# A hybrid decoder layer on one core: v after the scores, the first norm's place among the up products, and smaller moves

## The chip, the core and the metric

The kernel runs on one core of a Trainium2 chip. Its time is the device time of one execution in microseconds (us); of the three runs shown the median counts. The engines are TensorE (PE in the profile, with its weight loads as PEld), VectorE (DVE), ScalarE (ACT), GpSimd (POOL) and SyncE (SP), whose queue issues nearly all DMAs, in order. ACT, DVE and POOL, too, each run their instructions in the order in which the program gives them.

## The reference

One decoder layer for a prompt of 2048 tokens and 8 samples of 8 tokens: 2112 tokens of width 1024, in float32.

```python
# ada: scale, shift, gate for both norms from silu(c) @ w_ada
h = rmsnorm(x) * (1 + scale) + shift
qkv, z, b, a, sq, sk, sv = split(h @ w_in)        # one input projection
# (A) gated DeltaNet, 4 heads of 128: short causal conv, silu, q and k normalized,
decay = exp(G_i - G_j)                            # G: cumulated log decay
A = strict_lower(beta * (k @ k.T) * decay)        # scores k.k, and (q @ k.T) * decay
T = inverse(I + A)
u = T @ (beta * v) - T @ (beta * exp(G) * k) @ S  # state S goes from chunk to chunk
o = (q * exp(G)) @ S + (q @ k.T * decay) @ u
# (B) banded attention, window 128, with sinks and a position bias
x = x + gate * (concat(A, B) @ w_out)
h = rmsnorm(x) * (1 + scale2) + shift2
y = x + gate2 * ((silu(conv(h @ w_up_g)) * conv(h @ w_up_u)) @ w_down)
```

## The kernel before

A product in float32 is made of three products of halves: each factor is split into a rounded high part and the rest (hi and lo for the tokens, w_hi and w_lo for the weights), and `gemm_steps` adds hi·w_hi, lo·w_hi and hi·w_lo for eight k steps of 128, 24 matmuls in one PSUM bank (line 370 of the kernel; a matmul has up to 512 columns, the tokens). `split` (lines 361 and 362) casts the high part of a weight on ACT and subtracts for the low part, on DVE unless it is handed another engine. A weight piece w_raw of 512 KB has two buffers, and so have w_hi and w_lo: the next piece can only be loaded once the low part of the piece two before it is done.

The tokens are worked on in two halves, of two blocks of 512 and of blocks of 384, 384 and 320. In order of time the stages are: the ada modulations (`ada_cols`) and the input projection of the first half (`inproj`); the mixers of the first half, chunks of 128 tokens in four generators that advance side by side (`front` for the chunk two ahead, `levels` for the next, `scan` and `attend` for the chunk itself), with the input projection of the second half as a filler between their steps; `between(0)`, which is the output projection of the first half and its second norm; the mixers of the second half with the up-projection of the first as filler; the sample tokens (`sample_delta`, `sample_attend`); `between(1)`; the up-projection of the second half (`up_quarters`, a form with fewer products, whose weight sums are split in a ring of tiles); and the down-projection. `weight_sums` makes sums of pieces of the down weights for a product form with fewer products, from two loads of 512 KB, four additions of 128 by 512 and two stores (ws_d) for each of its eleven units; before, six run on POOL beside the input projection and five on DVE beside the sample tokens.

What sets the order: the generators say what is offered when (`beside(steps, filler, share)` takes `share` steps of the filler for each step), and a scheduler then puts every engine's instructions in one order. `tc.issue_after(x)` keeps what is issued inside it behind x.

`front` loads kq (keys and queries of a chunk) and xv (its values) from the tensor proj, to which the input projection stores through SP. It transposes kq for the squares (kq_ps), forms the decay Dc, transposes v and scales it to vb (lines 735 and 737), and then makes the scores AM (am_ps, two products of two heads each, and four operations on DVE), whose part AT is stored to at_d and read back as blocks G, from which DVE inverts 16 by 16 blocks. `levels` joins these to larger blocks, and `scan` reads vb.

A second norm goes through `ffn_in`: the squares are added up by token on ACT and POOL (line 1317, acc), `token_rstd` sums them over partitions on TensorE (ss_ps), takes the root (rsq on DVE, rtok on POOL), spreads it as diagonals (dg on DVE) and sends it back through TensorE (rb_ps), and `affine_h` scales the tokens and splits them into hi and lo (x at line 295, hi at 301 on ACT, lo at 302 on DVE and 299 on POOL). In the first half the norm of the last block runs beside the first up products, which use the other block.

In `between`, free PSUM banks are handed out in turn (`turns`), and `out_weights` keeps two split weights ahead of the output products.

## Time and profile before

| what | number |
|---|---|
| runs | 2584.51, 2585.77 and 2588.64 us, median 2585.77 |
| profiled execution | 2588.13 us, span 2586.4 us, mean granted clock of TensorE 0.994 |
| busy in the span | PE 97%, DVE 70%, ACT 50%, POOL 30% |
| input projection of the first half | up to about 242 us |
| mixers of the first half | about 387 to 745 us |
| output projection of the first half, norm | about 745 to 892 us |
| sample tokens | about 1290 to 1420 us |
| output projection of the second half | about 1531 to 1632 us |
| matmuls | 16410 |

Busy is the time in which an engine executes; a row of the timeline has the start in us, the duration, engine, line, operation and tiles, and in brackets the idle time of that engine before it with what ended it. Where an engine has no bracket, it did not wait. "x8" means that so many instructions are merged in the row. A granted clock of 0.50 in a stretch means that TensorE ran at half speed there.

### The profile page before, as it was taken

What the parts mean: (1) busy time and instruction counts of PE and PEld (TensorE: products, weight loads), DVE (VectorE), ACT (ScalarE), POOL (GpSimd) and SP (SyncE); (2) the same over time, 40 slices, a digit from 0 to 9 for tenths busy, and PEclk for the clock granted to TensorE, in tenths of its full rate; (3) what the DMA queues carried; (4) which work ended last, traced back from release to release, by engine and by line L of the source; (5) the groups of instructions that cost most, each with busy time, mean ns of one, the idle gap of its engine ahead of it and who ended that gap; (6) DMA issues with size and microseconds to landing.
All of it is one profiled execution on the core that took longest, in us unless ns stands there. A gap on an engine that the chain in (4) does not pass through costs nothing.

```text
span 2586.4 us, 45302 instructions
## 1 busy us (share of the span) xinstructions
PE 2515.8 (97%) x16410; PEld 2211.3 (85%) x16410; DVE 1811.4 (70%) x3621; ACT 1286.7 (50%) x3133; POOL 763.9 (30%) x697
## 2 busy tenths in 40 slices
PE   7999999999999999999999999999999999999998
PEld 5777888888988787787887789999999998888998
DVE  6465579897543677788758665886776666687676
ACT  5554365554343455465544353655555554454453
POOL 2064143323232422222111123345555520021012
PEclk9999999999999999999999999999999999999999
DMA  7887553343555353443346267325555448676463
GB/s 278 281 297 255 159 141 112 101 120 93 128 178 203 109 150 96 107 104 100 88 163 200 80 219 225 112 78 164 174 174 183 160 168 293 213 242 201 138 193 133
DMA packets 315852, 427.62 MB, mean 165 GB/s; under 512 B 82243, under 2 KB 206244, under 8 KB 315364
## 3 DMA queue, kind: packets, MB, share of 16 engines
q1 hardware_dynamic: 315052, 423.55, 51.8%
q8 instruction: 129, 2.11, 0.3%
q0 software_dynamic: 288, 1.11, 0.1%
q14 instruction: 95, 0.78, 0.1%
q10 hardware_dynamic: 288, 0.06, 0.0%
HBM read 305.07 MB, written 120.57 MB: 165 GB/s over the span
## 4 chain that ended last, share of the span: by engine, by line
PE 75%; DVE 11%; DMA 6%; ACT 3%; issue 2%; POOL 2%; SPq 1%; DVEq 0%; POOLq 0%; ACTq 0%
PE up_ps L370 19%; PE dn_ps L1850 17%; PE in_ps L370 8%; PE op_ps L370 6%; PE uq_b L1632 6%; PE uq_c L1632 3%; DVE ev L581 3%; PE uq_u L1632 2%; PE uq_g L1632 2%; PE uq_a L1632 1%; PE as_ps L1009 1%; DMA wada<-in_w_ada_dram 1%; PE pv_ps L1047 1%; PE u_ps L819 1%; DVE w_lo L362 1%
## 5 line engine op out<-in xcount | busy, mean ns | idle before, releaser
L370 PE MATMUL in_ps<-hi,w_hi 128*128 128x512 f32 (+2 forms) x880 | 319.4, 366 | 2.5 <-ACT hi L301 1.9
L370 PE MATMUL in_ps<-lo,w_hi 128*128 128x512 f32 (+2 forms) x880 | 315.6, 359 | 3.1 <-DVE lo L302 2.0
L370 PE MATMUL up_ps<-hi,w_hi 128*128 128x512 f32 (+2 forms) x808 | 313.0, 388 | 1.5 <-ACT sg L576 1.5
L370 PE MATMUL in_ps<-hi,w_lo 128*128 128x512 f32 (+2 forms) x880 | 314.0, 357 | 0.5 <-POOL w_lo L362 0.5
L370 PE MATMUL up_ps<-lo,w_hi 128*128 128x512 f32 (+2 forms) x808 | 312.1, 387 | 1.9 <-DVE lo L302 1.9
L370 PE MATMUL up_ps<-hi,w_lo 128*128 128x512 f32 (+2 forms) x808 | 311.0, 386 | 0.1
L1850 PE MATMUL dn_ps<-tl,wh 128*128 128x512 f32 (+2 forms) x796 | 271.6, 341 | 0.0
L1850 PE MATMUL dn_ps<-th,wh 128*128 128x512 f32 (+2 forms) x796 | 269.9, 341 | 0.0
L1850 PE MATMUL dn_ps<-th,wl 128*128 128x512 f32 (+2 forms) x796 | 268.7, 341 | 0.0
L361 ACT CAST w_hi<-w_raw 128x1024 fp32r<-128x1024 f32 x126 | 132.1, 1049 | 145.9 <-PE op_ps L370 63.0
L362 DVE TENSOR_TENSOR w_lo<-w_raw,w_hi 128x1024 fp32r<-128x1024 f32 x115 | 145.3, 1264 | 84.1 <-ACT w_hi L361 78.3
L370 PEld LDWEIGHTS in_ps<-lo,w_hi 128*128 128x128 f32 x880 | 166.9, 190 | 23.1 <-issue 3.4
L370 PEld LDWEIGHTS in_ps<-hi,w_hi 128*128 128x128 f32 x880 | 166.2, 190 | 23.2 <-issue 3.6
L370 PEld LDWEIGHTS up_ps<-hi,w_hi 128*128 128x128 f32 x808 | 152.3, 188 | 35.2 <-issue 7.3
L370 PEld LDWEIGHTS up_ps<-lo,w_hi 128*128 128x128 f32 x808 | 152.4, 189 | 33.4 <-issue 6.4
L370 PEld LDWEIGHTS in_ps<-hi,w_lo 128*128 128x128 f32 x880 | 166.5, 189 | 15.9 <-issue 1.0
L370 PEld LDWEIGHTS up_ps<-hi,w_lo 128*128 128x128 f32 x808 | 152.1, 188 | 27.9 <-issue 1.6
L1734 ACT CAST wh<-wr 128x512 fp32r<-128x512 f32 x149 | 92.2, 619 | 154.8 <-PE dn_ps L1850 101.6
L581 DVE SCALAR_TENSOR_TENSOR ev<-rb,cw,ev 128x512 f32<-128x512 f32 (+2 forms) x180 | 142.6, 797 | 35.2 <-ACT ev L574 31.5
L1850 PEld LDWEIGHTS dn_ps<-tl,wh 128*128 128x128 f32 x796 | 150.5, 189 | 15.7 <-DVE tl L1735 0.3
L1850 PEld LDWEIGHTS dn_ps<-th,wl 128*128 128x128 f32 x796 | 150.4, 189 | 15.2
L1850 PEld LDWEIGHTS dn_ps<-th,wh 128*128 128x128 f32 x796 | 150.2, 189 | 15.5
(574 smaller groups left out, 6414.6 us busy)
## 6 DMA issues: line engine op xcount, KB each, us to landing
w_raw<-in_w_upT_dram SPq DMA_DIRECT2D x50, 512.0 KB
wada<-in_w_ada_dram SPq DMA_DIRECT2D x48, 512.0 KB
w_raw<-in_w_inT_dram SPq DMA_DIRECT2D x44, 512.0 KB
wr<-ws_d SPq DMA_DIRECT2D x88, 256.0 KB
w_raw<-in_w_outT_dram SPq DMA_DIRECT2D x34, 512.0 KB
d<-act_d SPq DMA_DIRECT2D x33, 512.0 KB
wr<-in_w_downT_dram SPq DMA_DIRECT2D x66, 256.0 KB
proj<-ev SPq DMA_DIRECT2D x44, 256.0 KB
```

The costliest lines, as they stand in the source:

```text
L361: nc.scalar.copy(hi, raw)
L362: (eng or nc.vector).tensor_tensor(lo, raw, hi.bitcast(F32), ALU.subtract)
L370: nc.tensor.matmul(ps[:, :n], a[:, k, :], b[:, k, :n], start=first is not False and k == ks[0] and i == 0, stop=last is not False and k == ...
L581: nc.vector.scalar_tensor_tensor(out, src(j), w[:, j:j + 1], out, ALU.mult, ALU.add)
L819: mm = lambda out, a, b, r, c: nc.tensor.matmul(out, a, b, start=True, stop=True, tile_position=(r, c))
L1009: nc.tensor.matmul(banks[v][:, 256 * g:256 * g + 256 - P * k0], qs[:, 2 * (g0 + g) + v], t[:, v, :2 - k0].rearrange("p w j -> p (w j)"), s ...
L1047: mm = nc.tensor.matmul(pv_ps[64 * v:64 * v + 64, :], (vprev[0], vt if k0 else dv)[half][:, 64 * v:64 * v + 64], PT[v, half], start=half = ...
L1632: nc.tensor.matmul(bk[t][:, :nb], u[:, k], v[:, k], start=new and k == 0 and y == 0, stop=k == KG - 1 and y == 2, skip_group_check=True)
L1734: nc.scalar.copy(h, raw)
L1850: nc.tensor.matmul(acc[m, s][:, :n], w[q, i][a][:, c], th[b][:, v], start=new and i == 0 and y == 0, stop=i == KH - 1 and y == 2, skip_gro ...
```

## The change

Nothing that is computed changes. The edits are:

- `front`: the transposes of v and vb come after the scores, their store and the loads of G, instead of before them. The scheduler orders the mixers anew from that.
- `ada_init`: a Silu of 16 columns is issued first, so that ACT loads its table at the very start.
- `gates`: the exponential of al is issued behind the copy `held`.
- `weight_sums`: five units (FEW) on POOL beside the input projection and six on DVE beside the sample tokens.
- `between`: the output projection starts at the other bank (`turns[0] = 1`); in the first half, ss of the last block's norm stands behind six k steps (18 matmuls) of the up-projection and rb behind six more.
- `out_weights`: in the second half every second new split has its low part on POOL.
- `Quarters`: two further rings (RING_T) for the split weights instead of one; a copy of small constants becomes smaller for it.

On SP the first loads of kq move. Before, they stand here (the names are target and source of a DMA):

```order
L643 DMA proj<-ev 128x512 x2
L1685 DMA ws_d<-suv 128x1024 x2
L353 DMA w_raw<-in_w_inT_dram 128x1024
L691 DMA kq<-proj 128x4x128 x2
L693 DMA xv<-proj 128x4x128
```

and now:

```order
L360 DMA w_raw<-in_w_inT_dram 128x1024
L651 DMA proj<-ev 128x512
L699 DMA kq<-proj 128x4x128 x2
L701 DMA xv<-proj 128x4x128
L262 DMA he<-in_xT_dram 128x384 x2
```

The unit's stores ws_d are gone from ahead of kq, and the second of the two proj stores comes behind it; on TensorE the first kq_ps stands 33 matmuls of the input projection earlier.

On DVE the norm of the first half stood so, after the last split of the first up weights (sg and cv are conv taps of the up products):

```order
L581 SCALAR_TENSOR_TENSOR sg<-rb,fcw,sg 128x512 x2
L143 TENSOR_SCALAR rsq<-ss_ps 128x4
L599 SCALAR_TENSOR_TENSOR sg<-rb,sg 128x512
L223 TENSOR_SCALAR dg<-cst,rtok 128x128 x4
L581 SCALAR_TENSOR_TENSOR cv<-rb,fcw,cv 128x512 x2
L1350 SCALAR_TENSOR_TENSOR cv<-cv,sg 128x512
L295 SCALAR_TENSOR_TENSOR x_9223<-x_9223,MOD,rb_ps 128x512 x8
L302 SCALAR_TENSOR_TENSOR lo<-x_9223,MOD,hi 128x512 x2
```

and stands so now:

```order
L144 TENSOR_SCALAR rsq<-ss_ps 128x4
L230 TENSOR_SCALAR dg<-cst,rtok 128x128 x4
L589 SCALAR_TENSOR_TENSOR sg<-rb,fcw,sg 128x512 x2
L302 SCALAR_TENSOR_TENSOR x_9216<-x_9216,MOD,rb_ps 128x512 x3
L607 SCALAR_TENSOR_TENSOR sg<-rb,sg 128x512
L302 SCALAR_TENSOR_TENSOR x_9216<-x_9216,MOD,rb_ps 128x512 x5
L309 SCALAR_TENSOR_TENSOR lo<-x_9216,MOD,hi 128x512 x2
```

The norm's operations come ahead of the taps of the second up product, and of the first one's too. On TensorE, 36 up matmuls stood ahead of ss and 26 between ss and rb; now it is 18 and 18.

On POOL the start of the second half's output projection was only sums of squares (acc), the root and the token splits (lo):

```order
L1225 TENSOR_TENSOR mixl<-mt,mixh 128x320 x4
L1317 TENSOR_TENSOR acc<-acc,sq 128x384 x7
L144 TENSOR_TENSOR rtok<-rsq,mhalf 128x3
L1317 TENSOR_TENSOR acc<-acc,sq 128x384
L299 TENSOR_TENSOR lo<-ht,hi 128x384
```

Now the weight splits stand among them; this is its last third, from the root of the second block's norm on:

```order
L145 TENSOR_TENSOR rtok<-rsq,mhalf 128x3
L369 TENSOR_TENSOR w_lo<-w_raw,w_hi 128x1024
L1337 TENSOR_TENSOR acc<-acc,sq 128x320 x2
L369 TENSOR_TENSOR w_lo<-w_raw,w_hi 128x1024
L306 TENSOR_TENSOR lo<-ht,hi 128x384 x2
L1337 TENSOR_TENSOR acc<-acc,sq 128x320 x2
L306 TENSOR_TENSOR lo<-ht,hi 128x384
L369 TENSOR_TENSOR w_lo<-w_raw,w_hi 128x1024
L1337 TENSOR_TENSOR acc<-acc,sq 128x320
```

Nine splits of the output weights went from DVE's order to POOL's; a split stands ahead of the two lo's here.

The diff:

```diff
--- before.py
+++ after.py
@@ -4,6 +4,7 @@
 
 
 from contextlib import ExitStack, nullcontext
+from itertools import islice
 
 import numpy as np
 
@@ -154,6 +155,8 @@
         craw = tmp.tile([P, KT, 9], F32, tag="craw", name="craw")
         nc.scalar.dma_start(craw, I["cT"])
         cT = pool.tile([P, KT, 32], F32, tag="cT", name="cT")
+        warm = tmp.tile([P, 16], F32, tag="warm", name="warm")
+        nc.scalar.activation(warm, mhalf, AF.Silu)
         bT = pool.tile([P, 48], F32, tag="bT", name="bT")
         nc.vector.memset(cT, 0.0)
         nc.scalar.activation(cT[:, :, 0:9], craw, AF.Silu)
@@ -207,16 +210,20 @@
         yield True
 
 
+    asked = []
+
     def token_rstd(accs, n, dst, pool, bank):
 
 
         ps = bank("ss_ps")
         r = pool.tile([P, 4], F32, tag="rtok", name="rtok")
+        asked.clear()
 
         cuts = [min(t, n - P) for t in range(0, n, P)]
         for j, t in enumerate(cuts):
             for i, a in enumerate(accs):
-                nc.tensor.matmul(ps[:, j:j + 1], a[:, t:t + P], ones[:, 0:1], start=i == 0, stop=i == len(accs) - 1)
+                asked.append(nc.tensor.matmul(ps[:, j:j + 1], a[:, t:t + P], ones[:, 0:1], start=i == 0,
+                                              stop=i == len(accs) - 1).ins)
         rsqrt(pool, r[:, :len(cuts)], ps[:, :len(cuts)], 1.0 / D, len(cuts))
         dg = pool.tile([P, len(cuts), P], F32, tag="sq", name="dg", bufs=2)
         for j, t in enumerate(cuts):
@@ -224,7 +231,7 @@
         yield True
         bp = bank("rb_ps")
         for j, t in enumerate(cuts):
-            nc.tensor.matmul(bp[:, t:t + P], ones, dg[:, j], start=True, stop=True)
+            asked.append(nc.tensor.matmul(bp[:, t:t + P], ones, dg[:, j], start=True, stop=True).ins)
         if dst is not None:
             nc.scalar.copy(dst[:, :n], bp[:, :n])
         yield True
@@ -467,7 +474,7 @@
                     nc.tensor.matmul(pb[:32, :n], wb[:, k, :], h[bi][i][:, k, :n], start=i == 0 and k == 0,
                                      stop=i == 1 and k == KT - 1)
             ev = gw.tile([P, 512], F32, tag="cv", name="ba_ev", bufs=CV)
-            nc.scalar.copy(ev[:32, :n], pb[:32, :n])
+            held = nc.scalar.copy(ev[:32, :n], pb[:32, :n]).ins
             yield True
             ps = st_bank("bat_ps")
             for i, t in enumerate(range(0, n, P)):
@@ -484,7 +491,8 @@
         dt = pool.tile([P, H], F32, tag="dt", name="dt")
         nc.sync.dma_start(al, I["dn_A_log"][0].partition_broadcast(P))
         nc.sync.dma_start(dt, I["dn_dt_bias"][0].partition_broadcast(P))
-        nc.scalar.activation(al, al, AF.Exp)
+        with tc.issue_after(held):
+            nc.scalar.activation(al, al, AF.Exp)
         t0, t1, t2 = [pool.tile([P, NCH // 2 + 1, H], F32, tag=t, name=t)[:, :n_] for t in ("t0", "t1", "t2")]
         sl = slice(c1, c1 + n_)
 
@@ -730,13 +738,6 @@
             nc.vector.tensor_scalar_mul(nr[:rows, :, 0], nr[:rows, :, 0], 1.0 / f)
         nc.vector.tensor_scalar_mul(nr[:rows, :, 1], nr[:rows, :, 1], float(128.0 ** -0.5))
         yield True
-        v_ps = bank("v_ps", "fr")
-        for h in range(H):
-            nc.tensor.transpose(v_ps[:rows, P * h:P * h + P], xv[:, h, :], ident)
-        vb = pool.tile([P, H, P], F32, tag="vb", name="vb", bufs=two)
-        nc.vector.tensor_tensor(vb[:rows], heads(v_ps)[:rows], over_i(nr[:rows, :, 0], P), ALU.mult)
-        yield True
-
         AM = pool.tile([P, H, 2, rows], F32, tag="AM", name="AM", bufs=1 if smp else 2)
         for s in range(2):
             am_ps = bank(f"am_ps{s}", "fr")[:, :4 * rows].rearrange("p (h i t) -> p h i t", h=2, i=2)
@@ -759,6 +760,12 @@
         for h in range(H):
             nc.sync.dma_start(G[nb * h:nb * h + nb], bass.AP(a0.tensor, a0.offset + h * rows,
                                                              [[BS * ap_ + BS, nb], [ap_, BS], [1, BS]]))
+        yield True
+        v_ps = bank("v_ps", "fr")
+        for h in range(H):
+            nc.tensor.transpose(v_ps[:rows, P * h:P * h + P], xv[:, h, :], ident)
+        vb = pool.tile([P, H, P], F32, tag="vb", name="vb", bufs=two)
+        nc.vector.tensor_tensor(vb[:rows], heads(v_ps)[:rows], over_i(nr[:rows, :, 0], P), ALU.mult)
         yield True
         TU = pool.tile([4 * P // BS, 2, BS, BS], F32, tag="TU", name="TU", bufs=1)
         T0 = TU[:np_, 0]
@@ -1227,6 +1234,8 @@
 
 
 
+    FIRST_UP = (6, 6)
+
     OUT_ORDER = (tuple(range(KT)), (KT - 2, KT - 1, *range(KT - 3, -1, -1)), (1, 0, *range(2, KT)))
 
     def out_weights(hf):
@@ -1239,7 +1248,7 @@
                 del w[m]
                 new = next((x for x in seq[i + 1:] if x not in w), None)
                 if new is not None:
-                    w[new] = load_split(I["w_outT"][new])
+                    w[new] = load_split(I["w_outT"][new], nc.gpsimd if hf and i % 2 else None)
             yield
 
     def outproj(hf, bi, mix, sums, op, weights, kept=None):
@@ -1286,6 +1295,7 @@
         beside(chain(mix_load(hf, 0, mix, op), mix_load(hf, 1, mix, op)), filler, SHARE[4][hf])
         rest(filler)
         weights = out_weights(hf)
+        turns[0] = 1
         steps = outproj(hf, 0, mix, sums, op, weights)
         for bi in range(2, nb):
             beside(mix_load(hf, bi, mix, op), steps, 2)
@@ -1297,7 +1307,17 @@
             beside(ffn_in(hf, bi, h, sums, op), steps, SHARE[5])
             rest(steps)
         up = up_proj(hf, h, uc[0], op, ms)
-        beside(ffn_in(hf, nb - 1, h, sums, op, *kept), up, SHARE[6][hf])
+        normed = ffn_in(hf, nb - 1, h, sums, op, *kept)
+        if not hf:
+            next(normed)
+            rest(islice(up, FIRST_UP[0]))
+            with tc.issue_after(asked[-1]):
+                next(normed)
+                next(normed)
+                rest(islice(up, FIRST_UP[1]))
+            with tc.issue_after(asked[-1]):
+                beside(normed, up, SHARE[6][hf])
+        beside(normed, up, SHARE[6][hf])
         return up, h
 
     def residual(out, ps, n, np_, g, x, pool):
@@ -1425,7 +1445,7 @@
             halves_of("T4", b21, k)
             yield
 
-    RING, RING_T = 6, 1
+    RING, RING_T = 6, 2
 
     def quarter_tiles(pool, i):
         return [pool.tile([P, KG, P], F32R, tag=f"r{s}{i}", name=f"r{s}") for s in "hl"]
@@ -1433,7 +1453,8 @@
     def copy_consts(dst, src):
         for t in ("cw", "cb"):
             nc.gpsimd.tensor_copy(dst[t], src[t])
-        nc.gpsimd.tensor_copy(dst["out"][:, 2 * PLAIN:], src["out"][:, 2 * PLAIN:])
+        late = lambda a: a[:, a.shape[1] - MU + 2 * PLAIN:]
+        nc.gpsimd.tensor_copy(late(dst["out"]), late(src["out"]))
 
     class Quarters:
 
@@ -1927,6 +1948,7 @@
 
     SHARE = (5.4, 5.5, 4.0, 2.05, (2.0, 1.4), 5.0, (1.3, 2.0), 8.0)
     PLAIN = 3
+    FEW = 5
 
     gate = cp.tile([P, NCH + 1, H], F32, tag="gate", name="gate")
     ghl = cp.tile([P, 2, NCH + 1, H], F32R, tag="ghl", name="ghl")
@@ -2031,7 +2053,7 @@
         at_bank = lambda name: bank(name, "at")
         tasks = lockstep(
             chain(*[spaced(ada_cols([(c, k + q) for q in range(4)], ac, st, at_bank), 2) for c in range(2, 6) for k in (0, 4)],
-                  spaced(weight_sums(range(6), sa, nc.gpsimd), 2)),
+                  spaced(weight_sums(range(FEW), sa, nc.gpsimd), 2)),
             chain(bias_tables(sa), gates(0, h, ic["wb"], ip), *[x_rstd(1, bi, rBs[bi], sa, st_bank) for bi in range(3)]))
         zero_images(sa)
         filler = inproj(0, h, ic, range(2, 12), tags=("acc", "acc", "fr", "fr", "at"), turn=(0, 0), w0=w2)
@@ -2104,7 +2126,7 @@
         nc.sync.dma_start(O["p_ssm"].rearrange("h k v -> k h v"), state[0])
         with ExitStack() as es:
             sp = new_pool(es, "sp", side="right")
-            beside(lockstep(sample_delta(sp), sample_attend(sp), weight_sums(range(6, KH), sp, nc.vector)), filler, SHARE[2])
+            beside(lockstep(sample_delta(sp), sample_attend(sp), weight_sums(range(FEW, KH), sp, nc.vector)), filler, SHARE[2])
         with ExitStack() as es:
             up_tags[:] = FREE_TAGS
             filler, h = between(1, filler, es, range(2 * PLAIN))
@@ -2118,7 +2140,8 @@
                 ts = new_pool(es2, "ts", side="right")
                 beside(chain(token_sums(q, ts), W.first(PLAIN)), filler, SHARE[7])
                 rest(filler)
-            uc2 = {t: tq.tile(list(a.shape), F32, tag=f"u{t}", name=f"u{t}") for t, a in uc[0].items()}
+            shape = lambda t, a: [P, MU - 2 * PLAIN, 18] if t == "out" else list(a.shape)
+            uc2 = {t: tq.tile(shape(t, a), F32, tag=f"u{t}", name=f"u{t}") for t, a in uc[0].items()}
             copy_consts(uc2, uc[0])
             nc.sync.dma_start(O["ffn_conv"][:, :2 * PLAIN], uc[0]["out"][:, :2 * PLAIN])
             states.close()
```

## The prediction, made before the changed kernel was run

> **What bounds the kernel now.** I read the page first: its span and the busy shares.
>
> ```profile
> span 2586.4 us, 45302 instructions
> PE 2515.8 (97%) x16410; PEld 2211.3 (85%) x16410; DVE 1811.4 (70%) x3621; ACT 1286.7 (50%) x3133; POOL 763.9 (30%) x697
> ```
>
> TensorE is idle for 2586.4 − 2515.8 = 70.6 us in all. None of the edits removes a matmul, so whatever they win must come out of those 70.6 us, or out of matmuls that run at half clock behind a stall. Next I read the waits of TensorE; of that view these are three that the edits aim at (columns: waited for in total, times, the longest).
>
> ```profile
> PE kq_ps L705 <- DMA kq<-proj: 4.5, 1, 4.5
> PE op_ps L370 <- DVE w_lo L362: 2.4, 3, 1.3
> PE uq_b L1632 <- DVE rl L1488: 1.5, 1, 1.5
> ```
>
> At most 8.4 us can be won by these; two more stand in the timeline of the norm (1.49 and 1.91). Last, the table by stretches gives the stage of the first mixers, the one behind it, and the clock behind two of the stalls (columns: length, PE, PEld, DVE, ACT, POOL busy with counts, then the granted clock).
>
> ```profile
> 370.00:610.00 240.00, 221.45 (x1909) 200.21 (x1909) 208.72 (x604) 128.69 (x441) 77.32 (x79) 0.99 0.38 106
> 610.00:745.00 135.00, 135.00 (x1111) 126.61 (x1110) 72.07 (x227) 58.80 (x186) 33.98 (x36) 0.99 0.47 126
> 242.80:246.20 3.40, 3.40 (x13) 2.93 (x14) 1.46 (x3) 0.80 (x2) 0.00 (x0) 0.50 1.07 399
> 1072.20:1075.60 3.40, 3.40 (x10) 0.77 (x9) 3.30 (x17) 1.94 (x6) 2.66 (x3) 0.50 0.00 0
> ```
>
> Behind each of the two stalls TensorE ran 3.4 us at half clock, which costs 1.7 us more. From 370 to 610 it idles 240 − 221.45 = 18.55 us in many small waits; from 610 to 745, with the filler's last part, not at all.
>
> **The norm of the first half (next to the first up products).** Rows of the timeline of TensorE, POOL and DVE:
>
> ```profile
> 865.68 0.39 PE L370 MATMUL up_ps<-hi,w_hi 128*128 128x512 f32 x1
> 872.48 0.95 PE L219 MATMUL ss_ps<-ones,acc 128*128 128x1 f32 x8
> 879.41 1.05 PE L227 MATMUL rb_ps<-dg,ones 128*128 128x128 f32 x8
> 884.53 0.50 PE L370 MATMUL up_ps<-hi,w_hi 128*128 128x512 f32 x1 [1.49 <-ACT sg L576]
> 886.93 0.50 PE L370 MATMUL up_ps<-lo,w_hi 128*128 128x512 f32 x1 [1.91 <-DVE lo L302]
> 888.01 0.63 PE L370 MATMUL up_ps<-hi,w_lo 128*128 128x512 f32 x1
> 891.00 0.55 PE L370 MATMUL up_ps<-hi,w_hi 128*128 128x512 f32 x1
> 866.97 1.93 POOL L1317 TENSOR_TENSOR acc<-acc,sq 128x512 f32<-128x512 f32 x1 [4.81 <-ACT sq L1316]
> 875.14 0.88 DVE L223 TENSOR_SCALAR dg<-cst,rtok 128x128 f32<-128x128 f32 x4 [0.91 <-POOL rtok L144]
> 880.50 5.36 DVE L295 SCALAR_TENSOR_TENSOR x<-x,MOD,rb_ps 128x512 f32<-128x512 f32 x8 [0.60 <-PE rb_ps L227]
> 885.78 1.76 DVE L302 SCALAR_TENSOR_TENSOR lo<-x,MOD,hi 128x512 fp32r<-128x512 f32 x2
> ```
>
> From 865.68 to 872.48 stand 30 matmuls of 512 columns without a wait: one every 6.80/30 = 0.227 us. From 888.01 to 891.00 seven of them take 2.99 instead of 1.59 us: 1.4 lost to the clock. With 18 matmuls ahead of ss instead of 36, TensorE is there at 872.48 − 18 × 0.227 = 868.4; POOL ends the last sum at 868.9, so a new wait of 0.5 comes. ss to the end of dg took 876.02 − 872.48 = 3.54, so dg is done at 872.4. ss (0.95) and 18 more matmuls (4.1) put TensorE at rb at 874.0: no wait. The x operations follow 1.09 later, at 875.1 instead of 880.5. They take 5.36, one sg (0.7) is now among them, and the first lo (half of 1.76) is done at 882.0. rb (1.05) and the remaining 36 matmuls of the first token block last until 874.0 + 1.05 + 8.2 = 883.2, so lo is 1.2 early. The evacuation that held the bank (sg) is early too, since the fourth product now takes over a bank one product older. The gain is 1.49 + 1.91 + 1.4 − 0.5 = 4.3. Later lo's (spaced 0.9 on DVE against 0.68 per k step) may cost a little; I take **−4.0**, ends −4.7 and −2.5.
>
> **One unit of weight sums moved, and kq with it.** SP's timeline and the chain:
>
> ```profile
> 225.94 7.74 SPq L643 DMA_DIRECT2D proj<-ev  x2
> 236.86 1.47 SPq L691 DMA_DIRECT2D kq<-proj  x2
> 236.86 5.79 DMA kq<-proj
> 242.72 4.67 DMA proj<-ev
> 247.41 3.35 DMA kq<-proj
> 242.70 1.93 PE L705 MATMUL kq_ps<-cst,kq 128*128 128x128 f32 x8 [4.49 <-DMA kq<-proj]
> ```
>
> Before, kq stands in SP's queue behind a second proj store, two ws_d stores that wait for POOL, and a weight. Now it stands right behind the proj store that left at 225.94, and must wait for that store to land. A store took 4.67 and kq 5.79 or 3.35; with at least 2 us for a store in a quieter queue (an estimate from half of 4.67) kq lands between 231.6 and 236.4. But TensorE's order also has kq 33 matmuls earlier: it arrives at 238.2 − 33 × 0.227 = 230.7. So the wait is 0.9 to 5.7 us, in the middle 3.3 against 4.49. Half clock stays for a wait of some 2 us and more, as behind the stall ahead of 1072.2, which a row below shows to be 2.4. I take **−1.2**; the ends are −5.3 (wait 0.9, no half clock) and +1.2. The unit's four operations, 128 by 512 like vb's, go to DVE in the sample stage, where TensorE is busy 129.57 of 130 us:
>
> ```profile
> L737 DVE TENSOR_TENSOR vb<-v_ps,nr x17: 671/691/693, 263.1 to 1366.9; 128x512 f32<-128x512 f32 x16, 64x512 f32<-64x512 f32 x1
> 1290.00:1420.00 130.00, 129.57 (x749) 101.02 (x748) 93.70 (x202) 56.15 (x153) 19.83 (x14) 1.00 0.53 175
> ```
>
> 4 × 0.69 = 2.8 us of DVE with 36 free: 0; uncovered it would be 2.8.
>
> **Splits of the second half's output weights on POOL.**
>
> ```profile
> L362 POOL TENSOR_TENSOR w_lo<-w_raw,w_hi x11: 2374/2396/2795, 345.8 to 746.5; 128x1024 fp32r<-128x1024 f32 x11
> 1616.85 1.03 ACT L361 CAST w_hi<-w_raw 128x1024 fp32r<-128x1024 f32 x1
> 1618.88 3.34 POOL L299 TENSOR_TENSOR lo<-ht,hi 128x384 fp32r<-128x384 f32 x2 [3.20 <-ACT hi L298]
> 1626.03 1.05 ACT L361 CAST w_hi<-w_raw 128x1024 fp32r<-128x1024 f32 x1 [1.09 <-DMA w_raw<-in_w_outT_dram]
> 1628.95 0.41 PE L370 MATMUL op_ps<-mixh,w_lo 128*128 128x320 f32 x1
> SPq L294 <- POOL lo L299: 2.1, 1, 2.1
> ```
>
> Of the 2.4 that op_ps waited for w_lo, 0.42 is in the first half (below) and 2.0 here, in two waits; they should go, as DVE loses nine splits. But the last split is POOL's: its weight lands at 1626.0, w_hi ends at 1627.08, and 2.40 on POOL end at 1629.5, where TensorE used it at 1628.95. Also POOL's lo of 1618.88, for which SP's queue waits with ht ahead of that weight (the last row), now stands behind a split that starts at w_hi's end, 1617.88, and lasts to 1620.3: 1.4 later, and the weight as much. So the stage ends 0.5 to 1.9 later, though no wait before it is left; if the weight comes as much earlier as the waits removed, it ends 1.5 earlier. I take **+0.7**, ends −1.5 and +1.9.
>
> **The other edits.** The second split ring removes the 1.49 at uq_b, but DVE's sums on either side of that split are unmoved, so about half comes back: **−0.7** (−1.5 to 0). The first output product of a half in another bank no longer waits for ev, by the rows:
>
> ```profile
> 770.22 1.45 DVE L362 TENSOR_TENSOR w_lo<-w_raw,w_hi 128x1024 fp32r<-128x1024 f32 x1 [6.43 <-ACT w_hi L361]
> 771.72 0.70 PE L370 MATMUL op_ps<-mixh,w_lo 128*128 128x512 f32 x1 [0.42 <-DVE w_lo L362]
> ```
>
> TensorE can start when w_hi is there, which DVE's split needs too, so at 770.2 (ev would have been waited for until 770.56), but its third matmul still waits for w_lo until 771.7: **0** (−0.3 to 0). The early table load takes 1.28 us from ahead of the squares:
>
> ```profile
> 5.86 1.28 ACT L159 ACT_TABLE_LOAD   x1
> 14.87 1.23 DVE L362 TENSOR_TENSOR w_lo<-w_raw,w_hi 128x1024 fp32r<-128x1024 f32 x1 [2.80 <-ACT w_hi L361]
> 16.01 0.16 DVE L143 TENSOR_SCALAR rsq<-ss_ps 128x4 f32<-128x4 f32 x1
> ```
>
> But rsq stands behind a split whose weight sets its time, and DVE's order there is unchanged: **0** (−1.3 to 0). The load ahead of al hides under the same work: 0.
>
> **v behind the scores.**
>
> ```profile
> PE d_ps L724 <- ACT junk L708: 2.4, 1, 2.4
> ```
>
> The scores leave DVE 0.69 us earlier per chunk (vb's row above) and vb comes later, behind the store of AM and the loads of G that SP queues. Scan reads vb only after the levels of its chunk, so nothing should wait for it; if that cover were gone, one vb (0.69) and a transpose would be paid per chunk, 17 times. Yet the scheduler reorders hundreds of rows of the mixers, and who stands how close behind whom is drawn anew. The 18.55 us of small waits need not shrink: some readers come nearer to their writers, others go farther. I take **0**, with ends of ±5, a quarter of 18.55.
>
> **The sum** is −4.0 − 1.2 + 0.7 − 0.7 = −5.2. The profiled execution took 2588.13 (1.7 around the span) and would take 2582.9; it lies 2.4 above the median of 2585.77, and the time predicted is in terms of that median: 2580.5, rounded to **2580**.
>
> **Rivals.** *Given back*: POOL's splits cost the full 1.9 and kq waits as before: −4.0 + 1.9 − 0.7 = −2.8, 2583. For it: the last weight's landing at 1626; against: DVE's relief ahead of it. *More*: kq's wait shrinks to 0.9 (−5.3) and the mixers lose 5: −4.0 − 5.3 + 0.7 − 0.7 − 5 = −14.3, 2571.5. For it: SP's shorter queue; against: the store that must land first. *Slower*: the new order of the mixers makes long stalls like that of d_ps, each 2.4 and 1.7 of half clock, 4.1. It decides from three on: −5.2 + 12.3 = +7.1, 2593. For it: 18.55 us of waits show how tight the chains are; against: from 610 to 745 chains of the same kind cost no wait at all. *No half clock from short waits*: if only a stall of a whole 3.4 us closed the clock, kq's 3.3 would keep the full clock and win 1.7 more: 2578.5. The row at 1072.2, at 0.50 behind a stall of 2.4, speaks against it, and so do the seven slow matmuls behind stalls of 1.49 and 1.91. That is the rule of the Trainium skill, "TensorE: Matmul & The Clock Gate", Part 1: The HAM clock gate, half rate after at least one idle window of about 3.4 us. The length of the window agrees with the trace, the condition doesn't.
>
> **Chances and range.** Forecast 0.50, given back 0.22, more 0.10, slower 0.12, no half clock 0.06. This kernel's measurement tells 0.2%, 5.2 us, from no change; my sum lies on that line. Of the forecast a little over half is faster, the rest within: faster 0.28 + 0.10 + 0.05 = 0.43 and a part of *given back*, 0.46; slower 0.12; within 0.42. The forecast's own range is 2575 to 2586; with half of *more* and of *slower* it is 2570 to 2591.
>
> **What would show it.** Right: no wait for sg and lo near 884 and one of about 0.5 ahead of ss; kq still waiting 1 to 5 us at about 231; a wait for POOL's w_lo near the end of the second output projection; rsq of the start unmoved; 370 to 610 idle 14 to 23 us. Wrong, if that stretch changes by more than 5 us, or a stall over 3 us stands at a new place.

## The result, and the profile after

The changed kernel takes 2577.41 us (median of seven runs, 2575.84 to 2581.98), against 2585.77 us (seven runs, 2583.53 to 2588.85). The ratio is 0.996, with a 95% interval of 0.9947 to 0.9973: faster by 8 us, somewhat more than the predicted 5. The profiled execution, the fastest of the seven, took 2575.84 us, 12.3 less than that of before. From the page of the changed kernel, the span and the busy time:

```profile
span 2574.1 us, 45295 instructions
PE 2512.2 (98%) x16410; PEld 2208.6 (86%) x16410; DVE 1804.9 (70%) x3616; ACT 1284.1 (50%) x3131; POOL 780.7 (30%) x702
```

Idle time of TensorE is now 2574.1 − 2512.2 = 61.9 us, 8.7 less than before; the other 3.6 are busy time, matmuls that no longer run at half clock. The total is near the forecast, yet where it comes from is not. For the table I added up, stage by stage, the gaps between TensorE's instructions, and half of each stretch with a granted clock of 0.50 (the number behind the +).

| stage | before | after | change | predicted |
|---|---|---|---|---|
| start, up to 65 us | 18.25 + 1.71 | 17.92 + 1.71 | −0.3 | 0 |
| first input projection | 4.39 | 3.67 | −0.7 | 0 |
| from there over kq to the first mixers | 4.95 + 1.71 | 3.67 | −3.0 | −1.2 |
| mixers, first half | 19.28 + 3.41 | 12.17 | **−10.5** | 0 |
| output projection, first half | 2.26 + 1.71 | 1.59 | −2.4 | 0 |
| its norm | 3.40 + 1.71 | 1.92 | −3.2 | −4.0 |
| mixers, second half | 3.14 + 1.71 | 1.07 | **−3.8** | 0 |
| sample tokens | 0.43 | 1.63 | +1.2 | 0 |
| output projection, second half | 1.99 | 7.70 + 3.41 | **+9.1** | +0.7 |
| up-projection of the second half | 2.06 | 0.14 | −1.9 | −0.7 |
| down-projection | 3.38 + 5.44 | 3.38 + 5.23 | −0.2 | 0 |

The changes add up to −15.7, the spans differ by 12.3; half of a slow stretch is a rough measure, since TensorE also idles in it, and 3.4 us stay unplaced. The three bold rows are what I had not seen coming. The table by stretches shows them without the clock's part (columns: length, then busy time of PE, PEld, DVE, ACT and POOL with counts, granted clock, DMA share, GB/s). Before, first mixers, second mixers, second output projection:

```profile
296.00:768.00 472.00, 452.72 (x3726) 411.03 (x3725) 338.57 (x958) 241.31 (x760) 143.17 (x139) 0.99 0.45 127
909.00:1288.00 379.00, 375.86 (x2884) 301.90 (x2883) 305.74 (x857) 205.89 (x655) 84.27 (x80) 1.00 0.41 107
1506.00:1640.00 134.00, 131.96 (x755) 126.42 (x754) 93.59 (x135) 68.88 (x123) 53.82 (x43) 1.00 0.69 217
```

The same stages after:

```profile
280.00:755.00 475.00, 462.83 (x3757) 418.82 (x3750) 337.49 (x964) 245.36 (x767) 143.78 (x140) 1.00 0.46 130
894.00:1274.00 380.00, 378.93 (x2900) 306.01 (x2900) 308.58 (x866) 209.62 (x659) 87.00 (x78) 1.00 0.40 104
1485.00:1630.00 145.00, 137.31 (x760) 130.01 (x759) 94.40 (x128) 70.16 (x125) 72.44 (x53) 0.98 0.66 210
```

Length less PE's busy time is 19.3, 3.1 and 2.0 before, and 12.2, 1.1 and 7.7 after. In the last stage POOL is busy for 72 us instead of 54, which are the splits, but DVE, which gave them away, isn't busy for less (94.4 against 93.6 us): its other operations took longer. The timeline of that stage after shows what they met:

```profile
1559.88 2.35 POOL L369 TENSOR_TENSOR w_lo<-w_raw,w_hi 128x1024 fp32r<-128x1024 f32 x1
1562.18 1.00 POOL L1337 TENSOR_TENSOR acc<-acc,sq 128x384 f32<-128x384 f32 x1
1559.94 3.51 DVE L230 TENSOR_SCALAR dg<-cst,rtok 128x128 f32<-128x128 f32 x3 [0.97 <-POOL rtok L145]
1562.46 2.08 PE L234 MATMUL rb_ps<-dg,ones 128*128 128x128 f32 x6 [3.28 <-DVE dg L230]
```

DVE starts three dg of 128 by 128 at 1559.94, 0.06 behind POOL's split. One by one in the trace they take 2.37, 1.03 and 0.27 us: the first ends 0.08 after the split, the second 0.08 after the sum that follows on POOL. TensorE waits 3.28 us for the first, and at 1562.1, near the end of that wait, a half-clock stretch of 6.8 us begins. Two edits did about what they were meant to. First the norm of the first half, after:

```profile
853.59 1.05 PE L225 MATMUL ss_ps<-ones,acc 128*128 128x1 f32 x8 [0.38 <-POOL acc L1337]
858.74 1.05 PE L234 MATMUL rb_ps<-dg,ones 128*128 128x128 f32 x8
880.62 0.50 PE L377 MATMUL up_ps<-hi,mixh 128*128 128x512 f32 x1 [1.53 <-ACT sg L584]
865.71 1.41 DVE L309 SCALAR_TENSOR_TENSOR lo<-x,MOD,hi 128x512 fp32r<-128x512 f32 x2
868.74 3.48 DVE L309 SCALAR_TENSOR_TENSOR lo<-x,MOD,hi 128x512 fp32r<-128x512 f32 x2
868.68 2.99 POOL L306 TENSOR_TENSOR lo<-x,hi 128x512 fp32r<-128x512 f32 x2 [0.41 <-ACT hi L305]
```

The new wait ahead of ss is 0.38 (0.5 predicted), the wait for lo is gone, but that for sg stayed. The last two rows are the same meeting of DVE and POOL once more: two lo's on DVE take 3.48 us while POOL makes two of its own, and 1.41 just before. Then kq, after (SPq is the issue of a DMA):

```profile
225.54 0.92 SPq L699 DMA_DIRECT2D kq<-proj  x2
228.99 1.03 PE L713 MATMUL kq_ps<-cst,kq 128*128 128x128 f32 x8
235.43 0.50 PE L377 MATMUL in_ps<-hi,w_hi 128*128 128x512 f32 x1 [2.66 <-DVE ev L645]
```

TensorE takes kq without a wait; 6 us later it waits 2.66 us for an evacuation on DVE.

### The profile page after: what moved, and what is told of

It reads as the page before. It is cut to its first block, busy times and chain, and to the rows that moved or that the text cites. A ratio compares the mean times of both kernels' runs of the same rounds, so it can differ in the third digit from the quotient of the medians.

```text
span 2574.1 us, 45295 instructions
## 1 busy us (share of the span) xinstructions
PE 2512.2 (98%) x16410; PEld 2208.6 (86%) x16410; DVE 1804.9 (70%) x3616; ACT 1284.1 (50%) x3131; POOL 780.7 (30%) x702
## 4 chain that ended last, share of the span: by engine, by line
PE 73%; DVE 11%; DMA 7%; ACT 3%; issue 3%; POOL 2%; SPq 1%; POOLq 0%; DVEq 0%; ACTq 0%
PE dn_ps L1871 17%; PE up_ps L377 16%; PE in_ps L377 9%; PE uq_b L1653 6%; PE op_ps L377 5%; PE uq_c L1653 3%; DVE ev L589 3%; PE uq_u L1653 2%; PE uq_g L1653 2%; PE uq_a L1653 1%; DMA wada<-in_w_ada_dram 1%; PE as_ps L1016 1%; PE pv_ps L1054 1%; DMA mt<-mixd 1%; DVE w_lo L369 1%
## 5 line engine op out<-in xcount | busy, mean ns | idle before, releaser
L369 DVE TENSOR_TENSOR w_lo<-w_raw,w_hi 128x1024 fp32r<-128x1024 f32 x106 | 133.8, 1262 | 84.1 <-ACT w_hi L368 78.3
```

The source lines that it names most:

```text
L369: (eng or nc.vector).tensor_tensor(lo, raw, hi.bitcast(F32), ALU.subtract)
```

## The experiments

Two questions were open: why the splits on POOL cost 9 us, and why moving v won 14 in the mixers. In the expectations, A is the theory that an operation on POOL holds up those of DVE beside it; E, that the weight-sum unit ahead of kq sets kq's wait; G, that DVE's 0.69 us of vb ahead of the scores sets the mixers; H, that the PSUM bank which v takes ahead of them does. Kernels on one chip share the runs of before (medians 2592.22, 2587.86 and 2594.12 us on the three chips), so ratios and the idle time of stages are compared. "Mixers" below is idle time plus half of the half-clock stretches, both halves added: 27.5 before, 13.2 after.

**No splits on POOL** (from the changed kernel):

```diff
-                    w[new] = load_split(I["w_outT"][new], nc.gpsimd if hf and i % 2 else None)
+                    w[new] = load_split(I["w_outT"][new])
```

> The changed kernel with all low parts of the output weights back on DVE, nothing else undone. From the two traces, the stage of the second output projection lost 9 us of TensorE's time with the change (idle 7.7 instead of 2.0 us, and 3.4 us more at half clock). Theory A (a POOL split holds up DVE's operations on SBUF while it runs, and DVE then holds up TensorE): the whole loss goes, about 2568 to 2570 us. Rival B (the prediction's term: only POOL's own queue is late, 0.7 us): about 2576 to 2577. Either way the wait of 3.28 us for dg ahead of rb near 1562 us is the mark: gone by A.

2570.98 us, ratio 0.9929 (0.9907 to 0.9951). The second output projection idles 2.98 us, with no half clock. DVE's timeline in that stage of this kernel:

```profile
1554.41 0.68 DVE L230 TENSOR_SCALAR dg<-cst,rtok 128x128 f32<-128x128 f32 x3 [0.98 <-POOL rtok L145]
```

and the groups of DVE there (behind the bar the busy us and the mean ns of one, then the idle time before them):

```profile
L309 DVE SCALAR_TENSOR_TENSOR lo<-ht,MOD,hi 128x384 fp32r<-128x384 f32 x8 | 7.6, 974 | 0.0
L230 DVE TENSOR_SCALAR dg<-cst,rtok 128x128 f32<-128x128 f32 x6 | 1.4, 282 | 1.0 <-POOL rtok L145 1.0
```

The same groups with the splits on POOL, in the changed kernel:

```profile
L309 DVE SCALAR_TENSOR_TENSOR lo<-ht,MOD,hi 128x384 fp32r<-128x384 f32 x8 | 11.1, 1392 | 0.8 <-ACT hi L308 0.8
L230 DVE TENSOR_SCALAR dg<-cst,rtok 128x128 f32<-128x128 f32 x6 | 7.0, 1211 | 1.6 <-POOL rtok L145 1.6
```

And before the change:

```profile
L302 DVE SCALAR_TENSOR_TENSOR lo<-ht,MOD,hi 128x384 fp32r<-128x384 f32 x8 | 9.1, 1161 | 0.0
L223 DVE TENSOR_SCALAR dg<-cst,rtok 128x128 f32<-128x128 f32 x6 | 1.4, 281 | 1.0 <-POOL rtok L144 1.0
```

The same 128 by 128 operation takes 0.28 us alone and 1.21 in the mean beside the splits. The middle value of lo in before, 1161 ns, says that POOL's own lo's, too, hold up DVE: this could have been read before the change.

**dg of the second half on ACT**, splits still on POOL:

```diff
-            nc.vector.tensor_scalar_mul(dg[:, j], ident, r[:, j:j + 1])
+            spread(dg[:, j], ident, r[:, j:j + 1])
...
+                            nc.scalar.mul if hf else nc.vector.tensor_scalar_mul):
```

> The changed kernel with the splits left on POOL, but in the second half the diagonals dg of the norm are made on ACT instead of DVE. Theory A (DVE's dg, 0.28 us each before, is held up by the POOL split beside it until that ends, 2.37 us): the wait of 3.28 us ahead of rb shrinks below 1 us, since ACT isn't held up, and with it up to 3.4 us at half clock go: about 2572 to 2574 us; the waits for w_lo near 1614 us stay. Rival B (the root or POOL's queue is late, not DVE): rb still waits 3 us, about 2577 us.

2576.89 us, 0.9946 (0.9925 to 0.9967). The timeline of this kernel:

```profile
1565.33 2.36 POOL L369 TENSOR_TENSOR w_lo<-w_raw,w_hi 128x1024 fp32r<-128x1024 f32 x1
1565.39 0.99 ACT L230 ACTIVATE dg<-cst,rtok 128x128 f32<-128x128 f32 x3 [5.10 <-POOL rtok L145]
1565.85 1.07 PE L234 MATMUL rb_ps<-dg,ones 128*128 128x128 f32 x6 [1.21 <-ACT dg L230]
```

At the same place, 0.06 behind the start of POOL's split, ACT makes three dg in 0.99 us, and TensorE's wait falls from 3.28 to 1.21, a little more than the 1 us expected. So it is DVE that is held, not the data that is late. But dg is only some 2 us of the splits' cost: the stage loses 7.49 + 1.71 here against 7.70 + 3.41 in the changed kernel, since TensorE now waits for w_lo instead, 2.58 once for DVE's and four times, 3.7 in all, for POOL's. The wait of 2.58 is there in the changed kernel too, at 1614.33, and the same hold is a part of it. Rows of POOL and DVE in that kernel ahead of the split that came late:

```profile
1605.23 2.69 POOL L369 TENSOR_TENSOR w_lo<-w_raw,w_hi 128x1024 fp32r<-128x1024 f32 x1 [2.28 <-ACT w_hi L368]
1606.11 2.22 DVE L309 SCALAR_TENSOR_TENSOR lo<-ht,MOD,hi 128x384 fp32r<-128x384 f32 x1
1613.07 1.21 DVE L369 TENSOR_TENSOR w_lo<-w_raw,w_hi 128x1024 fp32r<-128x1024 f32 x1
```

The lo that meets POOL's split takes 2.22 us instead of 0.61, and DVE, busy all the way from there, comes to its own split 2.3 us after the w_hi for it was done (1610.80).

**Splits on POOL in the first block alone:**

```diff
-                    w[new] = load_split(I["w_outT"][new], nc.gpsimd if hf and i % 2 else None)
+                    w[new] = load_split(I["w_outT"][new], nc.gpsimd if hf and i % 2 and i < KT else None)
```

> The changed kernel with POOL splits only while the first block of the second half's output projection runs, before any norm's dg, x or lo are on DVE. Theory A (a POOL split costs what it holds up on DVE): nearly nothing there is held up but sums of residuals, so within 1.5 us of the run without POOL splits, idle of that stage 2 to 4 us. Rival (POOL splits are simply too slow at 2.4 us each): waits for POOL's w_lo of 0.2 to 1.2 us each at the three such splits, 1 to 3 us slower.

2575.33 us, 0.993 (0.9908 to 0.9952); the stage idles 4.36 us, with waits of 0.9 for dg and 0.8 for POOL's w_lo. It lies between the two: few splits cost less. That none are better than few is not shown by the times, since the interval overlaps that of the next two kernels.

**All lo's of the norms on DVE**, without splits on POOL, and beside it **no splits on POOL once more** (the first experiment's kernel again):

```diff
-        yield from affine_h(h[bi], bi, hf, 1, banks[1], src, smp=smp)
+        yield from affine_h(h[bi], bi, hf, 1, banks[1], src, pool_too=lambda k: 0, smp=smp)
```

> The changed kernel without POOL splits, and in both second norms POOL makes no lo either: all are DVE's (0.74 us each for 512 tokens, 0.6 for 384, when nothing runs beside them). Theory A carried on (POOL's lo's hold up DVE's operations too: two lo's took 3.48 us beside two POOL lo's at 868.7 us): the waits for sg at 881 (1.56 us) and for DVE's w_lo at 1574 and 1607 (1.35 and 1.33) shrink, 2 to 4 us in all against the run without POOL splits. Rival: DVE, which then has 12 more lo's of 0.6 to 0.74 us, becomes the late one; those waits stay or grow, 0 to 4 us slower than that run.

> The changed kernel without POOL splits once more, beside the two others on the same chip, for the comparison of versions: a ratio of 0.992 to 0.994 to the kernel before, as in its first run (0.9929); if its first run was a lucky execution, nearer 0.996, that of the changed kernel.

2570.3 us, 0.9918 (0.9891 to 0.9945), and 2571.28 us, 0.9914 (0.9892 to 0.9937). TensorE's timeline with the lo's on DVE:

```profile
880.44 0.50 PE L377 MATMUL up_ps<-hi,mixh 128*128 128x512 f32 x1 [0.49 <-ACT sg L584]
```

The wait for sg falls to 0.49, from 1.6 without splits on POOL (1.53 in the changed kernel), although DVE makes twice as many lo's. About half of that is DVE: counted from ss, its taps come 0.5 us earlier than in the changed kernel, now that no lo runs beside one of POOL's. The rest is the order on ACT, where the w_hi cast ahead of sg no longer stands behind a small copy that waits for DVE. The waits for DVE's w_lo in the second output projection were expected to shrink as well and did not (3.1 us in sum, against 3.0 and 4.0 without splits on POOL). The totals of the two kernels do not tell the 1 us at sg apart.

**v alone** (from the kernel before):

```diff
-        v_ps = bank("v_ps", "fr")
-        for h in range(H):
-            nc.tensor.transpose(v_ps[:rows, P * h:P * h + P], xv[:, h, :], ident)
...
         AM = pool.tile([P, H, 2, rows], F32, tag="AM", name="AM", bufs=1 if smp else 2)
...
+        v_ps = bank("v_ps", "fr")
+        for h in range(H):
+            nc.tensor.transpose(v_ps[:rows, P * h:P * h + P], xv[:, h, :], ident)
...
```

> The kernel before with one edit: v and vb behind the scores in front. In the two traces the first mixers (360 to 610 us) lost 21.5 us of TensorE's time before and 9.6 after, the second mixers 4.9 and 1.1. Theory C (the place of v makes that gain): idle from 360 to 610 falls to about 10 us, the time to about 2570 to 2574 us. Rival D (it comes from the other edits, which moved kq and all that follows): idle there stays at 17 to 21 us, about 2583 to 2587 us. The prediction's own view (drawn anew, 0 on average, ends of 5 us) stands between: 2581 to 2591 us.

2586.57 us, 0.9978 (0.9963 to 0.9994). The mixers fall from 27.5 to 17.4 (from 360 to 610 us TensorE idles 8.0, where C expected about 10), but the run wins only 5.6 us by medians, not the 12 to 16 that C would make of it. In its profile other stages give some of it back: the sample tokens 3.0, the up-projection of the second half 2.6, its output projection 1.4, kq 2.3, much of that in half-clock stretches at new places.

**v put back ahead of the scores**, all other edits in place; the edit is the same, the other way round:

> The changed kernel with v and vb back ahead of the scores, all other edits kept. Theory C (the place of v makes the mixers' gain of 12 to 16 us): idle from 350 to 610 us rises to 18 to 21 us, about 2589 to 2593 us. Rival D (the gain comes from the other edits): idle there stays near 10 us, about 2577 us. If both matter, 2580 to 2588 us.

2597.37 us, 1.0029 (1.0015 to 1.0043): slower than before the change. Without v's move the other edits together do not pay. The mixers take 31.9. From 350 to 610 us TensorE idles 13.2, less than the 18 to 21 expected; the second mixers, with 10.05 + 5.12, lose the more.

**The norm's edit alone** (from the kernel before):

```diff
...
+            with tc.issue_after(asked[-1]):
+                next(normed)
+                next(normed)
+                rest(islice(up, FIRST_UP[1]))
...
```

> The kernel before with one edit: ss of the first half's norm behind 18 up matmuls and rb behind 18 more. Prediction: the waits for sg (1.49 us) and lo (1.91) and the half clock behind them go, 0.5 us ahead of ss comes: 4 us, ratio 0.9985. In the changed kernel's trace a wait of 1.5 us for sg was left there, with no half clock. If the edit alone does that, idle plus half clock between 860 and 890 us falls from 5.1 to 1.9 us, ratio about 0.9988. If the mixers that follow are reordered by it, they move by up to 5 us on top, either way, and that shows in their idle time (6.5 us before), not here.

2599.96 us, 1.0046 (1.003 to 1.0061): slower too. The norm itself has the gain, 3.40 + 1.71 to 1.94 as in the changed kernel. But the second mixers go from 3.14 + 1.71 to 10.27 + 5.12. Their stretch in this kernel:

```profile
912.00:1309.00 397.00, 386.73 (x2920) 311.35 (x2919) 315.24 (x882) 211.20 (x674) 86.77 (x79) 0.99 0.38 102
```

and the waits of TensorE in it (total, times, longest):

```profile
PE p_ps L899 <- DVE xz L957: 5.9, 3, 4.3
PE z_ps L824 <- DMA T<-tu_d: 3.1, 2, 2.2
```

So an edit at 870 us makes a stall of 4.3 us at 1185 us: the scheduler draws the mixers behind it anew. That is the danger which the prediction priced as *slower*. The same stall of 4.3 to 4.4 us at p_ps stands in all three kernels that have this edit and v ahead of the scores in its own bank (this one, the one with v put back, and that one without splits on POOL), and in no other.

**Six units on POOL again**, all else as changed:

```diff
-    FEW = 5
+    FEW = 6
```

> The changed kernel with the sixth unit of weight sums back on POOL beside the input projection. Theory E (the unit's stores and POOL's additions ahead of kq in SP's queue made its wait): the first kq comes 8 to 14 us later again, with a wait of 3 to 5 us for its DMA, where the changed kernel had none there. Rival F (the earlier start of the stage, from the table loads, did it): kq stays at 229 us without a wait.

A single run, 2583.47 us. TensorE's timeline of this kernel:

```profile
245.11 1.97 PE L713 MATMUL kq_ps<-cst,kq 128*128 128x128 f32 x8 [4.41 <-DMA kq<-proj]
```

The wait is back, 16 us later than the changed kernel uses kq (8 to 14 were expected), and with it half clock from 244.1 on for 6.8 us. E holds: the moved unit removes the wait.

**G against H.** The first kernel makes Kt twice on DVE, which puts 0.69 us back ahead of the scores, with v behind (computing the same thing a second time); the second and third have v ahead again, with its product in another bank ("sc", the scan's) or in its own. None of the three makes output weight splits on POOL.

```diff
         nc.vector.tensor_tensor(Kt[:rows], kq_ps[0][:rows], over_i(bn[:rows, 1], P), ALU.mult)
+        nc.vector.tensor_tensor(Kt[:rows], kq_ps[0][:rows], over_i(bn[:rows, 1], P), ALU.mult)
```

```diff
+        v_ps = bank("v_ps", "sc")
+        for h in range(H):
+            nc.tensor.transpose(v_ps[:rows, P * h:P * h + P], xv[:, h, :], ident)
...
         AM = pool.tile([P, H, 2, rows], F32, tag="AM", name="AM", bufs=1 if smp else 2)
...
```

> The changed kernel with all splits on DVE (as in the run without POOL splits), and in front the operation that makes Kt issued twice: 0.69 us more on DVE ahead of the scores of each chunk, as vb was, without its PSUM bank and without transposes. Theory G (DVE time ahead of the scores is what v cost): the mixers' idle and half clock rise from 10.8 in the first and 3.6 us in the second half to 17 and 10 or so, 10 us or more in all. Theory H (the bank that v_ps took between d_ps and am_ps, and the waits by it, is what v cost): they stay within 4 us of 14.4 in sum.

> The same base, with v and vb ahead of the scores as before the change, but v_ps in another bank (that of the scan), so that am_ps no longer waits for vb by its bank; DVE still makes vb ahead of the scores. Theory G (DVE time): idle and half clock of the mixers rise to 25 us or more, as with v back in its own bank (33.8 us in both halves, against 15.2 in the changed kernel). Theory H (the bank): they stay near 15 us, unless the scan's single bank makes new waits at p_ps, which would show by name.

> The changed kernel without POOL splits and with v and vb ahead of the scores, v_ps in its old bank group: it differs from the run with v_ps in the scan's bank by that alone. Theory H (the bank between d_ps and am_ps is what v cost): idle and half clock of the mixers 25 to 38 us in sum, as in the other kernels with v ahead (27.6, 31.9, 38.2), against 19.0 with the other bank. If it is near 19, the bank is not the cause, and the other edits set how much v ahead costs.

A single run each: 2579.76, 2589.27 and 2587.02 us. The mixers take 14.6 with Kt twice, against 12.4 and 13.6 without, so G falls: the same 0.69 us of DVE in front of the scores cost 1 to 2, not 14. They take 19.1 with v ahead in the scan's bank and 36.0 in its own; 3.7 of the 36.0 are a wait at 757 us, just ahead of the output projection, and the half clock behind it. The mixers' stretches of the third, v ahead in its own bank:

```profile
284.00:762.00 478.00, 461.73 (x3760) 419.61 (x3760) 339.72 (x963) 245.20 (x767) 142.66 (x141) 0.99 0.46 129
899.00:1296.00 397.00, 387.48 (x2921) 312.14 (x2920) 316.96 (x884) 211.72 (x675) 86.88 (x79) 0.99 0.39 102
```

of the second, with v in the scan's bank:

```profile
285.00:759.00 474.00, 462.59 (x3776) 418.20 (x3770) 335.34 (x963) 244.90 (x767) 140.58 (x140) 1.00 0.46 129
899.00:1311.00 412.00, 404.29 (x3055) 323.81 (x3053) 328.16 (x901) 222.17 (x696) 89.64 (x82) 1.00 0.39 103
```

and the longest wait of the second mixers with v in its own bank, and what the same wait is in the scan's:

```profile
PE p_ps L901 <- DVE xz L959: 6.0, 4, 4.4
```

```profile
PE p_ps L901 <- DVE xz L959: 0.7, 1, 0.7
```

The first half is then as good as with v behind (11.4 idle, 12.2 after the change), and the half clock is gone from both; of the second half 7.7 us stay where v behind leaves 1.1. So it is the bank, and not DVE's time, that makes v ahead dear. Over all fourteen kernels the place of v tells the mixers apart without overlap: 27.5 to 38.2 in the four with v ahead in its own bank, 19.1 in the one with v in the scan's, 12.4 to 17.4 in the nine with v behind, whatever the other edits. How the bank does it can be seen in part in the kernel before. "fr" has two banks, and kq_ps (two), d_ps, v_ps and am_ps (two) take them in turn. Rows of TensorE and DVE for one chunk of before:

```profile
1081.29 0.60 PE L735 MATMUL v_ps<-cst,xv 128*128 128x128 f32 x4
1094.07 0.69 DVE L737 TENSOR_TENSOR vb<-v_ps,nr 128x512 f32<-128x512 f32 x1
1099.83 1.03 PE L744 MATMUL am_ps<-kq 128*128 128x256 f32 x4
```

v holds a bank for 13.5 us, from 1081.29 to 1094.76, and the scores come only behind it. That is a chunk of the second half. Medians of the eight chunks of each half:

| from, to | first half, before | after | second half, before | after |
|---|---|---|---|---|
| v's first transpose to the end of vb | 4.2 | 4.8 | 13.7 | 2.3 |
| first kq_ps to the end of AM | 35.7 | 29.9 | 41.9 | 40.9 |

In the first half, which won most, v holds its bank no longer before than after, but ahead of the scores, which are done 5.7 us earlier without it. In the second the hold shrinks by 11 us and the scores are done hardly earlier. And the kernel with v in the scan's bank has v ahead only in the program's text: v's first transpose stands behind the first scores in ten of the 16 chunks there, and in none of the 16 in the kernel with v ahead in its own bank. So that run shows that v's turn in the two banks keeps it ahead of the scores, and that the kernel is better without it; it does not show v ahead at no cost. By which waits the order then makes or removes a stall like p_ps's was not followed.

The totals of these three runs are not the sum of their parts: with v in the scan's bank the second output projection idles 9.04 + 1.71 though nothing is split on POOL there. Over all kernels without splits on POOL that stage idles 2.0 to 9.0 us (2.0, 3.0, 3.4, 4.0, 4.0, 3.2, 4.5, 5.0, 9.0), with all of them on POOL 7.5 to 8.3. The splits' cost of 7 to 8 us (11.1 against 3.0 and 4.0, half clock included) therefore rests on kernels whose mixers are alike (12.4 to 13.6: the changed kernel, the two without splits, and the one with dg on ACT), and on the rows of dg and lo.

**The version that beats both** is the changed kernel without the splits on POOL: 0.9929 and 0.9914 in two sessions, each on another chip, against 0.996 for the changed kernel on its own; on one chip it stood 5.9 us below the version with dg on ACT. Not tried alone were the early table load, the first output bank and the second ring.

## Why the prediction was right, and where it was not

The time, 2577.4, lies in the range and near the 2580 forecast, but by luck, as the sum of two misses of opposite sign, −14.3 in the mixers and +8.4 beyond the term for the splits. Both signs that I had named for being wrong were there: from 370 to 610 us TensorE idles 7.6 us instead of 18.55, and a stall above 3 us stands at a new place, 1562. Of the signs for being right, the small wait ahead of ss, the missing one for lo, POOL's w_lo late at the end of the stage (0.58) and an unmoved rsq (15.94, 16.01 before) came; the missing wait for sg, a wait for kq and 14 to 23 us from 370 to 610 did not. Term by term:

- **v behind the scores** (0 ± 5; measured −14.3 in the mixers, −10.1 with this edit alone). The step that failed is "who stands how close behind whom is drawn anew", which I took as chance without a sign. I counted DVE's 0.69 us per chunk, which the Kt experiment shows to be worth 1 to 2 us in all, and looked at who reads vb, but not at what v holds ahead of the scores: one of two banks, which they need next. The bank's list was in the kernel, and in the trace the time between v_ps and vb, 4 us in the median of the first half and 13.7 in the second.
- **Splits on POOL** (+0.7, −1.5 to +1.9; measured +9.1). The step that failed is "they should go, as DVE loses nine splits": the price was sought only at the end of the stage, on POOL and in SP's queue. What POOL takes it can take from DVE as well: dg took 2.37 us instead of 0.28, ending 0.08 after the split, and a lo 2.22 instead of 0.61. The page "SBUF — State Buffer" of the Trainium skill has a rule for it in the section "Who interferes with whom": DVE's second port pair is GpSimd's only one; `tensor_scalar` can contend for it in its two-port modes, where whoever issues first keeps it for the whole instruction, and so does an operation with two inputs in SBUF beside a GpSimd instruction that reads SBUF. The rows agree with that. By that rule the term would have been bounded, as an estimate, by a split's 2.35 us at each dg or lo that it meets, on the slow side. I had weighed the skill only on the clock. Besides the hold, POOL's own splits came late, 2.46 us each in the mean where DVE took 1.26 before.
- **The norm** (−4.0; measured −3.2, in its range). Right: the wait ahead of ss, rb without a wait, lo and the half clock gone. Wrong: "the evacuation that held the bank (sg) is early too". It stands on ACT behind a w_hi cast at 878.36 and behind taps on DVE, which POOL's lo's had held by some 0.5 us; without these lo's, and with another order on ACT, TensorE waits 0.49. What I could not have seen from this stage is that the edit alone lengthens the second mixers by 10.5 us.
- **kq** (−1.2, −5.3 to +1.2; measured −3.0 for the stage). "A store took 4.67 and kq 5.79 or 3.35" was too long for the quieter queue: kq was in use 3.45 us after its issue, with no wait. Not all of that was won, since 2.66 us came back at ev, without half clock. The stage lost 6.7 to 9.0 us (idle and half clock) in the four kernels with six units on POOL and 2.2 to 7.8 in the ten with five; the medians, 8.0 and 4.0, put the term at about −4.
- **The first output product** (0; measured −2.4). 0.67 of it is idle time; the rest is a half-clock stretch that did not open there, and that is chance: the version without splits on POOL had 1.63 + 1.71 there in one run and 1.99 in the other.
- **The second ring** (−0.7; measured −1.9). Half coming back was too careful; with two rings that stage idled 0 to 1.4 us over all kernels, with one 2.0 to 3.0.
- **The table loads** (0; start −0.3) as said; within what the start's idle time varies between kernels that are equal there (17.5 to 19.4 us).
- **Sample tokens** (0; measured +1.2): a gap of 1.61 ahead of pot_ps, for which the trace names no releaser. Every other version idles 1.4 to 2.2 us in this stage too, the one with the norm's edit alone among them, so it is neither the six units on DVE nor v's place; its cause stays open.

Of the rivals none came as written. *Slower* had the right mechanism at the wrong version: long stalls in the redrawn mixers decide the sign of the norm's edit alone (+12 us by medians). *More* had the right place, with gains at kq and in the mixers, but missed the size of both and the splits' cost, and was off by 6 us.

## What to carry to other kernels

Before work goes from DVE to POOL, list which DVE operations will run beside it: those from SBUF to SBUF can wait for the whole of POOL's instruction (2.37 us instead of 0.28 here), and a small one in a chain of waits is hurt most. Where a step moves ahead or behind in a chain, ask which buffers it holds meanwhile, not only how long it computes: here the turn of one product in two shared PSUM banks was worth some 14 us in the mixers, and the 0.69 us of DVE per chunk that went with it 1 to 2. And test edits in the company in which they will live: the norm's edit was worth −3 in its stage, and +12 in the whole while v still stood ahead.

## What the runs showed of the hardware

- A DVE operation of 0.28 us took 2.37 beside a POOL operation that had started 0.06 us earlier, and ended 0.08 us after it; a second one took 1.03 beside a sum on POOL. ACT made the three at the same place in 0.99 together.
- DVE's operations with an input in PSUM were not held: in the changed kernel none of them, of the forms that occur six times or more, took over 7% more than the median of its form. Beside a split on POOL there, one of them took 0.60 us, as elsewhere, and the next one, from SBUF alone, 1.36 instead of 0.21, ending 0.08 after the split:

```profile
1615.94 2.71 POOL L369 TENSOR_TENSOR w_lo<-w_raw,w_hi 128x1024 fp32r<-128x1024 f32 x1
1616.85 0.60 DVE L302 SCALAR_TENSOR_TENSOR ht<-ht,MOD,rb_ps 128x384 f32<-128x384 f32 x1
1617.37 1.36 DVE L1329 TENSOR_TENSOR x<-sres,x 128x64 f32<-128x64 f32 x1
```

- Whether a stall halves the clock does not follow from its length alone. Behind 2.66 us at 235.43 the clock stayed full after the change, while the 2.37 us of before (ahead of 1072) were followed by half clock. The table by stretches of the changed kernel, behind that stall and around the one of 3.28 us:

```profile
235.40:238.80 3.40, 3.38 (x15) 2.81 (x16) 3.40 (x6) 3.34 (x15) 1.44 (x1) 1.00 1.05 357
1562.10:1568.90 6.80, 6.35 (x21) 6.09 (x22) 6.80 (x12) 3.11 (x6) 3.46 (x4) 0.50 0.68 214
```

- At the start, where most versions are equal, the time at half clock differed from run to run between none and 10.2 us; the kernel without splits on POOL had 3.4 us there in one run and none in the other. The Trainium skill ("TensorE: Matmul & The Clock Gate", Part 1: The HAM clock gate) calls the window of 3.4 us free-running. The runs agree with that, but not with a whole idle window as the condition: 2.37 us were enough once, and 2.66 were not.
